# Two layers of attention and product-key experts: the expert gathers take the first four heads first, beside the selection of the other four

## The chip, the cores and the metric

One core of a Trainium2 chip runs the whole model. The metric is the time of one execution in device microseconds (us). The kernel before took 1806.02 us, the median of three runs between 1805.1 and 1806.14 us. TensorE is called PE (its weight loads PEld), VectorE DVE, ScalarE ACT, GpSimd POOL and SyncE SP; SP issues the weight loads, POOL the gathers.

## The reference

The input is one sequence of 256 tokens of 1024 numbers; 16 learned meta tokens are put ahead of it, so 272 tokens pass through two layers. A layer is a mixer (a causal convolution beside latent attention, merged by gates) and then a product-key expert layer:

```python
def _peer(h, wq, keys, u_table, v_table):          # h: 272 tokens after an RMS norm
    q = (hf @ wq).reshape(T, PEER_HEADS, 2, PEER_HALF)          # 8 heads, 2 halves of 128
    s = jnp.einsum('thpd,hpnd->thpn', q, keys)                  # 128 scores per half
    sv, si = lax.top_k(s, 16)
    cand = sv[:, :, 0, :, None] + sv[:, :, 1, None, :]          # 256 pairs
    top_s, top_pos = lax.top_k(cand.reshape(...), 16)           # 16 experts per head
    eidx = take(si[..., 0, ...] * 128 + si[..., 1, ...], top_pos)
    gw = softmax(top_s)
    # for each token its 128 experts:
    a = einsum('ted,td->te', u_table[eidx], x);  act = gelu(a) * gw
    out = einsum('te,ted->td', act, v_table[eidx])
```

There are 16384 experts, each a row of 1024 fp32 numbers in u_table and one in v_table, for each layer. The output is the 256 tokens without the meta tokens.

## The kernel before

**Stages.** In each layer the mixer comes first. Then 16 query tiles are made (the loop over i at L906): PE makes the queries and the scores, and DVE runs the top-16 (`top16`, L763) tile by tile beside it. The second selection (`second`, L807) turns the two sorted lists of a head into its 16 experts: a small table of candidate sums, a top-16 of it, a softmax on ACT, the place of each winner turned into a pair of list positions (L851 to L868, "pairs"), and two passes that look up the key numbers by those positions (L878 to L884, into `ef`). `heads(k, b)` (L887) does this for token block k (two blocks of 128 tokens) and heads 4b to 4b+3.

**Dense stages U and V.** 160 of the tokens are done densely. Stage U multiplies them by all 16384 rows of u_table: 128 stripes j of 128 experts, 8 matmuls of 128x160 each (`A<-xh,wraw`, which stand as 16 instructions on PE, two for an fp32 matmul); ACT and DVE turn `A` to the gated activation. Stage V multiplies by v_table, 128 stripes (`po<-X,wraw` and `po<-Xh,wraw`), accumulating the output. A weight tile of 1 MB holds two stripes; SP loads the tiles into a ring of four, and five tiles of U are loaded ahead during the query tiles (`we`). The last four stripes of V are done column block c by column block c (the tail); in layer 1 `turn_out` transposes each finished block and sends it out.

**Routes.** The gates of the dense tokens are a matrix of 160 tokens by 16384 experts, built on PE from one-hot matrices. The generator `routes` (L1045) makes their input beside U: w16 and its remainder at L1059 to L1061, and four transposes of `ef` on PE at L1072 for each token block k; `heads(1, 0)` and `heads(1, 1)`, the selection of the second token block, stand in it ("the second selection" below, whose transposes PE has in its queue at a fixed place). Then `wbuild` makes 40 blocks of `wp<-ohE,ohA`.

**Gathers.** The other 96 tokens, and in layer 0 the 16 meta tokens, are done by gathers. They stand in groups of 64, 32 and 16 tokens; a job is one expert of two heads for each of 64 tokens (of four heads for 32, of all eight for 16), 128 rows in all, so that there are 64 + 32 + 16 = 112 jobs in layer 0 and 96 in layer 1. `gather(k)` issues one indirect DMA from POOL (L1154): 128 rows of 8 KB, a u row and a v row of each expert, 1.05 MB into one of 4 buffers `gb`; its row numbers come from `iww`, which `spread` (L1035) writes from `ew` with a small DMA on POOL. Then DVE multiplies the u part by x with a running sum (L1182), ACT takes the gelu (L1192), DVE multiplies by the gate weight (L1161) and adds the v part times it (L1166), and the freed buffer takes the next gather. At the end `sum_heads` (L1024) sums the heads by PE with a matrix `zs`, and `put_back` adds to the residual `hT`.

**What sets the order.** Each engine executes its own instructions in the order in which the program is written. The two generators are advanced stripe by stripe: `routes` and `wbuild` by RB or RW[l] steps per stripe, the gathers by RU[l] steps per stripe of U from stripe J0 on (three steps per job), and in V by `rv`. In V a copy of one number of the newest weight tile (L1153, `warm`) stands ahead of each gather on POOL, so that a gather is issued no earlier than that tile has landed.

Of the kernel before, what the change touches and what calls it, by code (L numbers as in the profile page):

```python
# [7 lines left out]
F32 = mybir.dt.float32  # L8
# [11 lines left out]
META = 16  # L20
# [27 lines left out]
def trunk_kernel(ctx: ExitStack, tc: tile.TileContext, a: dict, out: bass.AP, dbg=None, stop=None):  # L48
# [135 lines left out]
    for l in range(NL):  # L184
# [622 lines left out]
        def second(v_, i_, nh, scale, iv, tsd):  # L807
# [47 lines left out]
            V.tensor_scalar(q3, po, 3, None, op0=OP.logical_shift_right)
            V.tensor_scalar(q2, po, 2, None, op0=OP.logical_shift_right)
            V.tensor_copy(nf, po)
            V.tensor_scalar(a_, q3, -1.0, 0.0, op0=OP.add, op1=OP.max)
            V.scalar_tensor_tensor(a_, q2, -5.0, a_, op0=OP.add, op1=OP.max)
            V.scalar_tensor_tensor(a_, nf, -42.0, a_, op0=OP.add, op1=OP.max)  # L860
# [116 lines left out]

        toks = [(META + sum(GROUPS[l][:g]), n) for g, n in enumerate(GROUPS[l])] + ([] if last else [(0, 16)])
# [17 lines left out]
        iww = [gp.tile([128, max(n // 16, 1), 2, min(n, 16)], F32, name=f"iww{i}") for i, (_, n) in enumerate(toks)]  # L996
        am = [gp.tile([128, max(n // 16, 1), min(n, 16)], F32, name=f"am{i}") for i, (_, n) in enumerate(toks)]
        zs_ = [gp.tile([128, n], F32, name=f"zs{i}") for i, (_, n) in enumerate(toks)]
        for z_, (_, n) in zip(zs_, toks):
            V.tensor_reduce(z_, ident.rearrange("p (t h) -> p t h", t=n), axis=AX.X, op=OP.add)  # L1000
# [34 lines left out]
        def spread(g):  # L1035

            q0, n = toks[g]
            s_ = done["e"][q0 - META:q0 - META + n]
            if n < 16:
                for q in range(2):  # L1040
                    G.dma_start(iww[g][:, 0, q], s_[:, :, q])
            else:
                G.dma_start(iww[g], s_)

        def routes():  # L1045
            done["e"] = ohp["ew"]
            spread(0)
            done["g"] = 1
            yield
            r2 = ohp["r"]  # L1050
            for k in range(2):
# [7 lines left out]
                V.tensor_scalar(h8(wh_), ts, WS, None, op0=OP.mult)  # L1059
                V.tensor_copy(ef[:, 2], wh_)  # L1060
# [82 lines left out]
        def gathers():  # L1143
# [52 lines left out]
            yield  # L1196
            yield
            sum_heads(len(toks) - 1)
            yield
            put_back(len(toks) - 1)  # L1200
# [56 lines left out]
        left = 3 * nj + 4 - done["n"]  # L1257
# [132 lines left out]
```

## Time and profile before

| | |
|---|---|
| median of 3 runs | 1806.02 us (1805.1 to 1806.14) |
| profiled execution | 1805.74 us, span 1804.0 us, mean granted clock 0.992 |
| PE busy | 1763.3 us, 98% |
| DVE busy | 1147.6 us, 64% |
| ACT, POOL busy | 422.7 us (23%), 329.3 us (18%) |
| U of layer 0 starts, V of layer 0 ends | 304 us, 928 us |
| U of layer 1 starts | 1202.65 us |
| DMA queue of the weights (q1), of the gathers (q0) | 338.54 MB, 218.35 MB |

The span is the time from the first to the last recorded instruction; the execution's own time is 1.7 us more. A PE that shows busy is not PE at its peak: matmuls whose weights come late are recorded as longer. The rows below are read with their columns as the line ahead of each group says; "[2.97 <-DVE ef L884]" means that the engine stood idle for 2.97 us and that DVE's instruction at L884 which writes `ef` ended it.

### The profile page before, as it was taken

What the parts mean: (1) busy time and instruction counts of PE and PEld (TensorE: products, weight loads), DVE (VectorE), ACT (ScalarE), POOL (GpSimd) and SP (SyncE); (2) the same over time, 40 slices, a digit from 0 to 9 for tenths busy, and PEclk for the clock granted to TensorE, in tenths of its full rate; (3) what the DMA queues carried; (4) which work ended last, traced back from release to release, by engine and by line L of the source; (5) the groups of instructions that cost most, each with busy time, mean ns of one, the idle gap of its engine ahead of it and who ended that gap; (6) DMA issues with size and microseconds to landing.
All of it is one profiled execution on the core that took longest, in us unless ns stands there. A gap on an engine that the chain in (4) does not pass through costs nothing.

```text
span 1804.0 us, 29548 instructions
## 1 busy us (share of the span) xinstructions
PE 1763.3 (98%) x11611; PEld 1627.8 (90%) x11611; DVE 1147.6 (64%) x3155; ACT 422.7 (23%) x1257; POOL 329.3 (18%) x393
## 2 busy tenths in 40 slices
PE   9999999989999999999999999999999999999998
PEld 7677888989999889988996878899899999999998
DVE  5577358997898654454535774587878886444341
ACT  3343112334444100000024331132344431000000
POOL 0121010222111223222200220102211122222220
PEclk9999999989999999999999999999999999999999
DMA  6223454889999999999962224658899999999994
GB/s 229 71 94 105 151 212 173 331 339 422 420 420 421 420 421 415 421 421 409 422 247 76 94 94 149 239 198 343 335 421 421 420 420 416 420 413 413 393 419 157
DMA packets 80684, 559.38 MB, mean 310 GB/s; under 512 B 9177, under 2 KB 12121, under 8 KB 13081
## 3 DMA queue, kind: packets, MB, share of 16 engines
q1 hardware_dynamic: 49488, 338.54, 47.5%
q0 software_dynamic: 30336, 218.35, 29.7%
q8 instruction: 91, 1.49, 0.3%
q10 hardware_dynamic: 720, 0.60, 0.1%
q14 instruction: 49, 0.39, 0.1%
HBM read 556.18 MB, written 1.05 MB: 309 GB/s over the span
## 4 chain that ended last, share of the span: by engine, by line
PE 72%; DMA 15%; DVE 7%; issue 5%; POOL 1%; ACT 0%; SPq 0%; DVEq 0%; POOLq 0%; ACTq 0%
PE po L56 23%; PE z L56 21%; PE A L56 19%; DMA wraw<-vn 10%; PE aps L56 5%; DMA wraw<-u 3%; PE wp L56 2%; DMA gb<-uv,iww 1%; DVE va L1166 1%; DVE gb L1182 1%; DVE ex L883 1%; DMA iww<-ew 0%; PE xp L56 0%; DMA wraw<-w_in 0%; DVE ex L880 0%
## 5 line engine op out<-in xcount | busy, mean ns | idle before, releaser
L56 PE MATMUL A<-xh,wraw 128*128 128x160 f32 x3776 | 540.6, 302 | 3.4 <-DMA wraw<-u 2.1
L56 PEld LDWEIGHTS A<-xh,wraw 128*128 128x128 f32 x3776 | 521.2, 191 | 6.4 <-DMA wraw<-u 3.4
L1182 DVE SCALAR_TENSOR_TENSOR gb<-gb,xr 128x1024 f32<-128x1024 f32 x208 | 254.6, 1224 | 344.3 <-DMA gb<-uv,iww 343.9
L56 PE MATMUL z<-xg,wraw 128*128 128x272 f32 (+1 forms) x1408 | 337.3, 394 | 0.8 <-DMA wraw<-w_in 0.7
L56 PEld LDWEIGHTS z<-xg,wraw 128*128 128x128 f32 x1408 | 265.4, 192 | 58.5 <-issue 7.5
L1154 POOL DMA_INDIRECT gb<-uv,iww x208 | 218.4, 1050 | 542.1 <-DVE va L1166 382.4
L56 PE MATMUL po<-Xh,wraw 128*128 128x160 f32 x2080 | 289.9, 300 | 9.3 <-DMA wraw<-vn 6.9
L56 PEld LDWEIGHTS po<-Xh,wraw 128*128 128x128 f32 x2080 | 283.4, 190 | 14.6 <-DMA wraw<-vn 11.2
L56 PE MATMUL po<-X,wraw 128*128 128x160 f32 x2016 | 280.3, 300 | 7.0 <-DMA wraw<-vn 5.6
L56 PEld LDWEIGHTS po<-X,wraw 128*128 128x128 f32 x2016 | 274.5, 190 | 12.3 <-DMA wraw<-vn 10.6
L1166 DVE SCALAR_TENSOR_TENSOR va<-gb,am,va 128x1024 f32<-128x1024 f32 x203 | 261.2, 1287 | 7.2
L1192 ACT ACTIVATE am<-am 128x1 f32<-128x1 f32 x208 | 41.4, 199 | 595.5 <-DVE gb L1182 595.3
L1093 ACT ACTIVATE ohA<-ohE,wlo 128x128 f16<-128x128 f16 x320 | 105.4, 427 | 7.8 <-DVE ohE L1090 5.6
L593 POOL TENSOR_TENSOR acc<-acc,cp 128x272 f32<-128x272 f32 (+1 forms) x60 | 51.1, 852 | 276.7 <-ACT cp L592 274.4
L1153 POOL COPY warm<-wraw 1x1 f32<-1x1 f32 x91 | 41.1, 452 | 289.3 <-DMA wraw<-vn 289.2
L585 DVE SCALAR_TENSOR_TENSOR acc<-upad,cols,acc 128x272 f32<-128x272 f32 (+1 forms) x180 | 83.8, 523 | 0.2
L1090 DVE TENSOR_TENSOR ohE<-ioh,idxT 128x512 f16<-128x512 f16 x160 | 60.4, 419 | 0.0
L56 PE MATMUL z<-xh,wraw 128*128 128x272 f32 (+1 forms) x256 | 57.3, 386 | 0.0
L56 PEld LDWEIGHTS z<-xh,wraw 128*128 128x128 f32 x256 | 48.6, 190 | 8.3
L1104 ACT ACTIVATE Xh<-wp 128x260 f32<-128x260 f32 (+17 forms) x80 | 25.7, 321 | 118.7 <-DVE Xh L1101 96.5
L56 PE MATMUL wp<-ohE,ohA 128*128 128x128 f16 x640 | 49.7, 218 | 0.0
L56 PEld LDWEIGHTS <-ohA 128*128 128x128 f16 x640 | 43.3, 97 | 3.0
(310 smaller groups left out, 1401.7 us busy)
## 6 DMA issues: line engine op xcount, KB each, us to landing
wraw<-vn SPq DMA_DIRECT2D x128, 1024.0 KB
wraw<-u SPq DMA_DIRECT2D x118, 1024.0 KB
wraw<-w_in SPq DMA_DIRECT2D x27, 1024.0 KB
wraw<-wq SPq DMA_DIRECT2D x16, 1024.0 KB
we<-u SPq DMA_DIRECT2D x10, 1024.0 KB
wraw<-w_out SPq DMA_DIRECT2D x8, 1024.0 KB
wraw<-w_mla SPq DMA_DIRECT2D x4, 1024.0 KB
wraw<-w_conv SPq DMA_DIRECT2D x4, 1024.0 KB
```

The lines of the kernel that those rows point to most:

```text
L56: PE.matmul(o, l, r, start=start, stop=stop, skip_group_check=True)
L585: V.scalar_tensor_tensor(acc[:, c, t0:], u_, weight(c, k), acc[:, c, t0:], op0=OP.mult, op1=OP.add)
L593: G.tensor_tensor(acc[:, 0, t0:], acc[:, 0, t0:], u_[:, t0:], op=OP.add)
L883: V.tensor_tensor(e3[:, :, 0:n], e3[:, :, 0:n], e3[:, :, n:2 * n], op=OP.add)
L1090: V.tensor_tensor(E[q], ioh[:, None].to_broadcast(full), pairs(q, b), op=OP.is_equal)
L1093: S.activation(A_[1][:, t // 2, :, t % 2], E[0][:, t // 2, :, t % 2], AF.Copy, scale=wlo[:, 4 * b + t:4 * b + t + 1])
L1104: S.activation(x_, p[:, :, a:b].rearrange("p t j -> p j t"), AF.Copy, scale=1.0 / WS)
L1153: G.tensor_copy(warm[0:1], state["w"][0:1, 0:1])
L1154: G.indirect_dma_start(out=g_, out_offset=None, in_=a[f"uv{l}"], in_offset=bass.IndirectOffsetOnAxis(ap=iww[i].bitcast(I32)[:, m // 16, 0, ...
L1166: V.scalar_tensor_tensor(vac[i], r, m_, vac[i], op0=OP.mult, op1=OP.add)
L1182: V.scalar_tensor_tensor(u_, u_, 1.0, xrs[i], op0=OP.mult, op1=OP.mult, accum_out=m_)
L1192: S.activation(m_, m_, AF.Gelu_apprx_tanh)
```

## The change

- The address list `iww` becomes permanent and is written in halves. Heads 0 to 3 (`numbers(.., 0)`, `spread(0, 0)`) are written ahead of the last scores. The rows of a job are arranged anew, so that the first half of a group's jobs (0 to 31 of the first 64) needs these heads only, the second half heads 4 to 7.
- `heads(0, 1)`, the eight small DMAs of the meta tokens (mv, mi), the addresses of heads 4 to 7 and four late top-16 (`behind`) move into `routes`, beside U.
- J0 goes from 8 to 3, RB from 0.75 to 0.85, RW from (0.52, 0.47) to (0.54, 0.5).
- The pairs are computed in ten DVE instructions instead of seventeen, on fp16.
- The gate multiply of a job goes from DVE to ACT, w16 and its fp32 copy too. The `zs` sums are made once at the start.
- The gathers are spread to the end of V, the last three stripes before the tail taking a job each. The last `sum_heads` and `put_back` stand in the tail ahead of block 5 (layer 0) or 1 (layer 1). `turn_out` of a block comes one block later.

```diff
-J0 = 8
+J0 = 3
-RB = 0.75
-RW = (0.52, 0.47)
+RB = 0.85
+RW = (0.54, 0.5)
...
-            V.tensor_copy(ab[0].rearrange("p h s -> p (h s)"), a_)
-            V.tensor_scalar(m, a_, 1.0, None, op0=OP.add)
-            V.scalar_tensor_tensor(m, a_, 2.0, m, op0=OP.mult, op1=OP.min)
-            w = ts
-            for d in (5.0, 17.0, 42.0):
-                V.tensor_scalar(w, a_, d, None, op0=OP.add)
-                V.scalar_tensor_tensor(m, m, 2.0, w, op0=OP.mult, op1=OP.min)
-            V.tensor_tensor(ab[1].rearrange("p h s -> p (h s)"), nf, m, op=OP.subtract)
...
+            W_.scalar_tensor_tensor(m, a_, 1.0, a_, op0=OP.min, op1=OP.add)
+            W_.scalar_tensor_tensor(m, m, 4.0, m, op0=OP.min, op1=OP.add)
+            W_.scalar_tensor_tensor(m, m, -4.0, nf, op0=OP.mult, op1=OP.add)
+            W_.tensor_scalar(b_, m, 0.0, None, op0=OP.max)
...
+        def numbers(ew, ef, x):
+            h4 = lambda q: ef[:, q, 64 * x:64 * x + 64].rearrange("p (h s) -> p h s", h=4)
+            V.scalar_tensor_tensor(ew.bitcast(I32)[:, 4 * x:4 * x + 4, 0], h4(0), 128.0, h4(1), op0=OP.mult, op1=OP.add)
+        def spread(g, x):
+            q0, n = toks[g]
+            G.dma_start(iww[g][:, n // 32 * x:n // 32 * (x + 1)], ohp["ew"][q0 - META:q0 - META + n, 4 * x:4 * x + 4])
...
+        run_all(early)
+        numbers(ohp["ew"], ohp["ef"], 0)
+        spread(0, 0)
         scores(15, pend)
-        if not last:
-            mv = rpool.tile([128, 1, 2, 16], F32, name="mv")
...
-                    G.dma_start(d4, s_[32 * q:32 * q + 16])
-        run_all(early)
-        run_all(heads(0, 1))
...
-        top16(behind[0:1])
-        top16(behind[1:2])
-        top16(behind[2:3])
-        top16(behind[3:4])
...
         def routes():
-            done["e"] = ohp["ew"]
-            spread(0)
+            r2 = ohp["r"]
+            if not last:
+                mv = rpool.tile([128, 1, 2, 16], F32, name="mv")
...
+                        G.dma_start(d4, s_[32 * q:32 * q + 16])
+            yield from heads(0, 1)
+            numbers(ohp["ew"], ohp["ef"], 1)
+            spread(0, 1)
+            for g in range(1, len(GROUPS[l])):
+                spread(g, 0)
+                spread(g, 1)
             done["g"] = 1
             yield
+            for b_ in behind:
+                top16([b_])
+                yield
...
-                V.tensor_scalar(h8(wh_), ts, WS, None, op0=OP.mult)
-                V.tensor_copy(ef[:, 2], wh_)
+                S.activation(h8(wh_), ts, AF.Copy, scale=WS)
+                S.activation(ef[:, 2], wh_, AF.Copy)
...
-                V.tensor_mul(m_, m_, iww[i][:, m // 16, 1, s_:s_ + 1])
...
                 S.activation(m_, m_, AF.Gelu_apprx_tanh)
+                S.activation(m_, m_, AF.Copy, scale=iww[i][:, m // 16, 1, m % 16:m % 16 + 1])
...
-        left = 3 * nj + 4 - done["n"]
         LJ = 128 - 2 * LASTP
-        rv = left / (LJ - 2)
+        tail = 3
+        rv = (3 * nj + 3 - done["n"] - 3 * tail) / (LJ - tail)
...
-            some_gathers(rv)
+            some_gathers(rv if j < LJ - tail else 3)
...
         for c in range(8):
+            if c == (1 if last else 5):
+                sum_heads(len(toks) - 1)
+                put_back(len(toks) - 1)
...
-                if c:
-                    turn_out(c - 1)
+                if c > 1:
+                    turn_out(c - 2)
                 V.tensor_add(hT[:, c, d0:], hT[:, c, d0:], pov[c])
         if last:
+            turn_out(6)
             turn_out(7)
```

POOL's queue at the start of U in layer 0. Before (mv and mi are the meta tokens' lists, iww0 the addresses of the first 64 tokens, gb a gather's buffer):

```order
L953 DMA mv_2102<-svm_1498 64x1x16 [waits DVE_49]
L953 DMA mi_2103<-sim_1499 64x1x16 [waits DVE_49]
L953 DMA mv_2102<-svm_1498 64x1x16
...
L1043 DMA iww0_2227<-ew_1823 128x1x128 [waits DMAHW1_49,DMAHW2_49,DMAHW0_49,DMAHW4_49,DMASW0_49,DMAHW7_49,DVE_49,Pool_49]
L1154 DMA gb_2260<-uv0,iww0_2227 128x2048 [waits DMASW1_49,DMASW0_49]
L1154 DMA gb_2262<-uv0,iww0_2227 128x2048 [waits DMASW2_49]
```

After, at the same place:

```order
L923 DMA iww0_1512<-ew_1832 128x1x64 [waits DVE_49]
L1043 DMA mv_2139<-svm_1504 64x1x16 [waits DVE_49]
L1043 DMA mi_2140<-sim_1505 64x1x16 [waits DVE_49]
...
L1158 DMA gb_2163<-uv0,iww0_1512 128x2048 [waits DMAHW2_49,DMAHW1_49,DMAHW4_49,DMAHW0_49,DMAHW7_49,DMASW1_49,Pool_49]
L1158 DMA gb_2165<-uv0,iww0_1512 128x2048 [waits DMASW2_49]
...
L923 DMA iww0_1512<-ew_1832 128x1x64 [waits DMASW5_49,DVE_49]
```

The first half of the addresses went ahead of the meta tokens' DMAs and the second half behind the first four gathers.

DVE's queue at the end of the selection of heads 4 to 7 of the first token block, in layer 0. Before (sv and si are top-16 lists):

```order
L883 TENSOR_TENSOR ex_2189<-ex_2189 128x4x32
L884 TENSOR_TENSOR ef_1822<-ex_2189 128x64
L958 SCALAR_TENSOR_TENSOR ew_1823<-ef_1822 128x8x16
L766 MAX sv_1496<-wlo_116 128x8
L768 MATCH_REPLACE idxT_115<-sv_1496,wlo_116 128x128
L770 MAX_INDEX si_1497<-sv_1496,wlo_116 128x8
```

After:

```order
L888 TENSOR_TENSOR ef_1831<-ex_2273 128x64
L1183 SCALAR_TENSOR_TENSOR gb_2163,am0_2116<-gb_2163,xr_2245 128x1024
L882 TENSOR_TENSOR ex_2289<-io16_96,ab1_2234 128x1024
...
L888 TENSOR_TENSOR ef_1831<-ex_2289 128x64
L918 SCALAR_TENSOR_TENSOR ew_1832<-ef_1831 128x4x16
L1183 SCALAR_TENSOR_TENSOR gb_2165,am0_2116<-gb_2165,xr_2245 128x1024
L1167 TENSOR_SCALAR va_2323<-gb_2163,am0_2116 128x1024
L771 MAX sv_1502<-wlo_122 128x8
```

Products of gathers now stand between the two look-up passes. Counted over DVE's whole queue of layer 0, 11 products stood ahead of the end of the second selection before and 17 stand there now; in layer 1 it was 11 and is 16.

PE's queue in U of layer 0, where the transposes of the second selection's ef stand. Before (stripes are 16 rows, A their sums):

```order
L56 MATMUL A_2919<-xh_1506,wraw_2718 128x160 x8
L56 MATMUL A_2919<-xh_1506,wraw_2818 128x160 x16
L1072 MATMUL wp_2953<-ident_89,ef_2517 128x128 x4
L56 MATMUL A_2961<-xh_1506,wraw_2855 128x160 x16
L56 MATMUL A_2961<-xh_1506,wraw_2904 128x160 x8
```

After:

```order
L56 MATMUL A_2977<-xh_1515,wraw_2858 128x160 x16
L56 MATMUL A_3012<-xh_1515,wraw_2915 128x160 x8
L1076 MATMUL wp_3023<-ident_89,ef_2626 128x128 x4
L56 MATMUL A_3012<-xh_1515,wraw_2915 128x160 x8
L56 MATMUL A_3012<-xh_1515,wraw_2958 128x160 x8
```

The four transposes moved from behind stripe 36 to behind stripe 43; in layer 1 from 37 to 44. The gather that comes last in layer 1 waits for the V tile of stripes 116 and 117.

## Rows read from the trace of the kernel before

**Rows 1.** Waits: engine, waiter, what ended it; total us, times, longest us.
```profile
DVE gb L1182 <- DMA gb<-uv,iww: 343.9, 155, 7.4
```

**Rows 2.** Windows of layer 0: us, each engine's busy us, PEclk, DMA share, GB/s.
```profile
304.00:313.00 9.00, 8.66 (x64) 8.69 (x65) 8.83 (x70) 2.92 (x6) 4.28 (x8) 1.00 0.54 210
313.00:327.00 14.00, 14.00 (x107) 14.00 (x106) 13.00 (x57) 0.62 (x1) 0.58 (x1) 1.00 0.70 236
327.00:345.00 18.00, 18.00 (x136) 18.00 (x135) 15.61 (x74) 10.83 (x19) 7.28 (x7) 1.00 0.92 370
345.00:400.00 55.00, 48.69 (x338) 47.82 (x337) 52.40 (x185) 17.50 (x37) 12.84 (x10) 0.91 0.89 335
...
500.00:600.00 100.00, 99.51 (x803) 97.46 (x803) 86.18 (x189) 38.90 (x138) 19.31 (x20) 1.00 1.01 420
...
901.00:928.00 27.00, 27.00 (x204) 27.00 (x203) 5.55 (x13) 3.00 (x7) 0.00 (x0) 1.00 0.59 220
```

**Rows 3.** Timeline of PE in V: start, us, instruction, count, idle before.
```profile
645.17 4.61 PE L56 MATMUL po<-X,wraw 128*128 128x160 f32 x32 [0.35 <-DMA wraw<-vn]
...
900.25 13.31 PE L56 MATMUL po<-Xh,wraw 128*128 128x160 f32 x96 [0.36 <-DMA wraw<-vn]
...
928.22 7.04 PE L56 MATMUL z<-xg,wraw 128*128 128x272 f32 x30
```

**Rows 4.** Timeline of POOL: the addresses and gathers of both layers.
```profile
311.44 0.61 POOL L953 DMA_DIRECT2D mi<-sim  x1
322.31 0.58 POOL L1043 DMA_DIRECT2D iww<-ew  x1 [10.26 <-issue]
327.40 1.03 POOL L1154 DMA_INDIRECT gb<-uv,iww  x1 [4.52 <-DMA iww<-ew]
...
883.08 0.96 POOL L1154 DMA_INDIRECT gb<-uv,iww  x1 [1.64 <-DVE va L1166]
...
888.04 0.96 POOL L1154 DMA_INDIRECT gb<-uv,iww  x1 [1.63 <-DVE va L1166]
...
1225.72 1.00 POOL L1154 DMA_INDIRECT gb<-uv,iww  x1 [3.54 <-DMA iww<-ew]
```

**Rows 5.** Timeline of PE at the second selection's transposes, both layers.
```profile
389.19 0.48 PE L1072 MATMUL wp<-ident,ef 128*128 128x128 f32 x1 [2.97 <-DVE ef L884]
392.13 0.80 PE L1072 MATMUL wp<-ident,ef 128*128 128x128 f32 x2 [2.46 <-DVE ef L1060]
392.72 9.00 PE L56 MATMUL A<-xh,wraw 128*128 128x160 f32 x48
...
1288.36 0.47 PE L1072 MATMUL wp<-ident,ef 128*128 128x128 f32 x1 [2.76 <-DVE ef L884]
1289.91 0.80 PE L1072 MATMUL wp<-ident,ef 128*128 128x128 f32 x2 [1.07 <-DVE ef L1060]
1290.50 11.14 PE L56 MATMUL A<-xh,wraw 128*128 128x160 f32 x64
```

**Rows 6.** Windows behind the stall of layer 0, columns as in rows 2.
```profile
390.00:396.00 6.00, 3.87 (x15) 3.73 (x16) 5.86 (x14) 1.41 (x5) 1.73 (x2) 0.50 0.83 315
396.00:399.00 3.00, 3.00 (x19) 3.00 (x18) 2.96 (x8) 1.36 (x5) 1.82 (x2) 0.76 0.63 213
```

**Rows 7.** Timeline of DVE, the first of the seventeen instructions of the pairs.
```profile
312.21 0.19 DVE L855 TENSOR_SCALAR q<-po 128x64 int32<-128x64 int32 x1
```

**Rows 8.** Groups by line: out<-in, count; busy us, mean ns; idle before.
```profile
L1161 DVE TENSOR_TENSOR am<-am,iww 128x1 f32<-128x1 f32 x208 | 32.2, 155 | 0.4 <-ACT am L1192 0.4
```

**Rows 9.** Timeline of DVE in layer 1: end of heads 0 to 3, first product.
```profile
1204.06 0.22 DVE L884 TENSOR_TENSOR ef<-ex 128x64 f32<-128x64 f16 x1
...
1234.37 1.23 DVE L1182 SCALAR_TENSOR_TENSOR gb<-gb,xr 128x1024 f32<-128x1024 f32 x1 [6.50 <-DMA gb<-uv,iww]
```

**Rows 10.** Timeline of PE in the tail of layer 1: the first and last of four.
```profile
1787.36 1.35 PE L56 MATMUL po<-Xh,wraw 128*128 128x160 f32 x8 [0.41 <-DVE hT L1298]
...
1797.96 1.35 PE L56 MATMUL po<-Xh,wraw 128*128 128x160 f32 x8 [0.69 <-DVE hT L1298]
```

**Rows 11.** Page: busy us, share of the span and instructions of each engine.
```profile
PE 1763.3 (98%) x11611; PEld 1627.8 (90%) x11611; DVE 1147.6 (64%) x3155; ACT 422.7 (23%) x1257; POOL 329.3 (18%) x393
```

More of the change, by code (lines that the diff above doesn't have):

```diff
@@ L141, in trunk_kernel @@
     V.memset(ec[0:8, 1:2], 0.0)
+    zs_ = {}
+    for n in (64, 32, 16):
+        zs_[n] = pp.tile([128, n], F32, name=f"zs{n}")
+        V.tensor_reduce(zs_[n], ident.rearrange("p (t h) -> p t h", t=n), axis=AX.X, op=OP.add)
     idxT = pp.tile([128, 3, 256], F16, name="idxT")
@@ L850, in second @@
             S.activation(tsd, ce, AF.Exp, scale=scale)
-            q3, q2, nf = rt("q3", [nh * 16], I32), rt("q2", [nh * 16], I32), rt("nf", [nh * 16])
-            a_, m = rt("ra", [nh * 16]), rt("rm", [nh * 16])
+            q3, q2 = rt("q3", [nh * 16], I32), rt("q2", [nh * 16], I32)
+            nf, m = rt("nf", [nh * 16], F16), rt("rm", [nh * 16], F16)
             ab = [rt(f"ab{p}", [nh, 16], F16) for p in range(2)]
[L855 to L860, printed above, removed]
-            V.tensor_copy(ab[0].rearrange("p h s -> p (h s)"), a_)
-            V.tensor_scalar(m, a_, 1.0, None, op0=OP.add)
-            V.scalar_tensor_tensor(m, a_, 2.0, m, op0=OP.mult, op1=OP.min)
-            w = ts
-            for d in (5.0, 17.0, 42.0):
-                V.tensor_scalar(w, a_, d, None, op0=OP.add)
-                V.scalar_tensor_tensor(m, m, 2.0, w, op0=OP.mult, op1=OP.min)
-            V.tensor_tensor(ab[1].rearrange("p h s -> p (h s)"), nf, m, op=OP.subtract)
+            a_, b_ = [x.rearrange("p h s -> p (h s)") for x in ab]
+            W_ = V
+            W_.tensor_scalar(q3, po, 3, None, op0=OP.logical_shift_right)
+            W_.tensor_scalar(q2, po, 2, None, op0=OP.logical_shift_right)
+            W_.tensor_copy(nf, po)
+            W_.tensor_scalar(a_, q3, -1.0, 0.0, op0=OP.add, op1=OP.max)
+            W_.scalar_tensor_tensor(a_, q2, -5.0, a_, op0=OP.add, op1=OP.max)
+            W_.scalar_tensor_tensor(a_, nf, -42.0, a_, op0=OP.add, op1=OP.max)
+            W_.scalar_tensor_tensor(m, a_, 1.0, a_, op0=OP.min, op1=OP.add)
+            W_.scalar_tensor_tensor(m, m, 4.0, m, op0=OP.min, op1=OP.add)
+            W_.scalar_tensor_tensor(m, m, -4.0, nf, op0=OP.mult, op1=OP.add)
+            W_.tensor_scalar(b_, m, 0.0, None, op0=OP.max)
             yield
@@ L905, in trunk_kernel @@
         early = heads(0, 0)
+        toks = [(META + sum(GROUPS[l][:g]), n) for g, n in enumerate(GROUPS[l])] + ([] if last else [(0, 16)])
+        iww = [pp.tile([128, n // 16, 2, 16], F32, name=f"iww{i}") for i, (_, n) in enumerate(toks)]
+        def numbers(ew, ef, x):
[4 more added lines that the diff above has]
+            G.dma_start(iww[g][:, n // 32 * x:n // 32 * (x + 1)], ohp["ew"][q0 - META:q0 - META + n, 4 * x:4 * x + 4])
         behind = []
@@ L976, in trunk_kernel @@
         n0 = 256 - N
-        toks = [(META + sum(GROUPS[l][:g]), n) for g, n in enumerate(GROUPS[l])] + ([] if last else [(0, 16)])
         xs_ = ExitStack()
@@ L994, in trunk_kernel @@
         xrs, vac = {}, {}
[L996 to L1000, printed above, removed]
+        am = [gp.tile([128, n // 16, 16], F32, name=f"am{i}") for i, (_, n) in enumerate(toks)]
         as2 = ExitStack()
@@ L1028, in sum_heads @@
             for c in range(8):
-                mm(done["p"][:, c], vac[i][:, c * 128:(c + 1) * 128], zs_[i], True, True)
+                mm(done["p"][:, c], vac[i][:, c * 128:(c + 1) * 128], zs_[n], True, True)
         def put_back(i):
@@ L1033, in put_back @@
             V.tensor_tensor(h_, h_, done["p"], op=OP.add)
[L1035 to L1043, printed above, removed]
-        def routes():
-            done["e"] = ohp["ew"]
-            spread(0)
+        def routes():
+            r2 = ohp["r"]
+            if not last:
+                mv = rpool.tile([128, 1, 2, 16], F32, name="mv")
+                mi = rpool.tile([128, 1, 2, 16], U32, name="mi")
+                for q in range(4):
+                    for d_, s_ in ((mv, svm), (mi, sim)):
+                        d4 = d_.rearrange("(n x) o s b -> x n o s b", x=2)[q // 2, :, 0, q % 2]
+                        G.dma_start(d4, s_[32 * q:32 * q + 16])
[5 more added lines that the diff above has]
+                spread(g, 1)
             done["g"] = 1
             yield
-            r2 = ohp["r"]
+            for b_ in behind:
+                top16([b_])
+                yield
             for k in range(2):
@@ L1169, in gathers @@
                 gather(k)
-            for g in range(1, len(GROUPS[l])):
-                spread(g)
             yield from x_steps(0)
@@ L1195, in gathers @@
             add(*prev)
[L1196 to L1200, printed above, removed]
         b_ = bg()
```

6 lines of the change are left out of this document (removed).

## The prediction

> **What bounds the kernel now.** I read the waits first. The largest wait that leads anywhere is VectorE's, 344 us over 155 products, for the rows of a gather to land [rows 1]. Then the windows of layer 0 from the start of stage U (304 us) to the end of V (928 us): in 500 to 600 us the DMA engines are fully used at 420 GB/s [rows 2]. The reader is to see that in these windows the engines are full from about 400 to 901 us and not full at both ends, at 210, 236, 370 and 335 GB/s ahead of it and 220 behind it. Third, the PE rows: while gathers run, two stripes of V cost 4.61 us and 0.35 us of waiting for a weight tile, without gathers six cost 13.31 us, 2.2 each [rows 3]. In 4.96 us one weight tile of 1.05 MB lands, 211 GB/s, and one gather of 1.05 MB is issued per 4.96 us [rows 4]: the two streams halve the 420. So layer 0 from 304 to 928 us is a number of bytes at 420 GB/s plus two stretches where too little is asked for. Layer 1 has 16 gathers fewer and no such full stretch early on; there PE is the bound, and only what idles PE counts.
>
> What delays the gathers is the fourth view. Their addresses, iww, were written at 322.31 us and the first was issued at 327.40 us in layer 0, at 1225.72 us in layer 1 [rows 4], because the selection of all eight heads stood ahead. Fifth, PE idles at the second selection's transposes: 2.97 and 2.46 us in layer 0, 2.76 and 1.07 in layer 1, always for VectorE's ef, and the 48 and 64 matmuls behind take 9.00 and 11.14 us instead of 6.6 and 8.8 [rows 5]. The granted clock there is 0.50, the 1.2 GHz level, in 390 to 396 us, and 0.76 in the next 3 us [rows 6].
>
> **Part 1, the early gathers in layer 0.** Against 420 GB/s the windows lack 9 x 210 = 1.89 MB, 14 x 184 = 2.58, 18 x 50 = 0.90 and 55 x 85 = 4.68 MB: together 10.05 MB, or 23.9 us of the DMA engines' time [rows 2]. After the change the addresses of heads 0 to 3 need only the first head group. The DMA that writes them is issued first on POOL; behind it, ahead of the first gather, stand the eight small DMAs of the 16 meta tokens, the last of which went out at 311.44 us and took 0.61 us [rows 4]. They keep their place because they wait for a top-16 that is not moved. So the first gather goes out at 312.1 us, 15 us earlier, and the window 313 to 327 looks like the present ramp of 327 to 345. Bounds for the saving: if everything from 327 us on stays as it is, the new deficit is 1.89 + 0.7 + 0.90 + 4.68 = 8.2 MB and 1.9 MB (4.5 us) is saved; if the engines are full from 313 us on, it is 1.9 MB and 8.2 MB (19.4 us) is saved. The order gives the middle: 17 products instead of 11 stand ahead of the end of the second selection. Six more gathers of 1.05 MB are 6.3 MB, 15.0 us. I take 15.0, the value nearest the order; it asks that VectorE does the six within about the same time. VectorE is busy 52.4 of 55 us in 345 to 400 [rows 2], so the six (about 2.7 us each with product and add) are paid from what goes: the three sums, two of three w16 steps, seven instructions of about 0.19 us in each of three calls of the pairs [rows 7], the gate multiply of 0.155 us per job [rows 8], some 7 us in all, and the idle time ahead of 345 us (1.0 + 2.4 us [rows 2]).
>
> The end of V gives the other part. Before, the last gather went out at 888.04 us [rows 4], the engines stayed full to 901 us, and 12 stripes were left from there to 928.22 us [rows 3] at 220 GB/s: 27 x 200 = 5.4 MB not asked for. After, the last gather waits for the tile of stripes 116 and 117. It is now issued with 17 stripes left (12 from 901 us, and about 5 in 13 us at 2.5 each), then with about 12: its rows land some 7 stripes from the end, about 17 us, a deficit of 3.4 MB. That saves at most 2 MB, 4.8 us; the last add, the sum over heads and its add now stand in the tail ahead of block 5 and may wait for it, so I take 3 us between 0 and 4.8. PE's stall in layer 0 is no term of its own: while PE stood, the ring of tiles filled and the engines' shortage is in the 4.68 MB. Layer 0: -18.0 us.
>
> **Part 2, layer 1.** Transposes of the second selection move from stripe 37 to 44. Without the waits PE would reach them at 1290.50 - 3.83 + 7 x 2.2 = 1302 us [rows 5]. VectorE: heads 0 to 3 are finished at 1204.3 us [rows 9]; from the issue of the addresses' DMA to the first gather it took 5.1 us in layer 0 (322.31 to 327.40), and from there to the first product 8.65 us in layer 1 (1225.72 to 1234.37) [rows 4, 9], so the first product can stand at 1218.0 us. The sixteenth is 15 x 4.96 us behind, and with 3 us, an estimate, for the selection's last steps the matrix is ready at 1295.4 us: 6.6 us ahead of PE. So the stall of 2.76 + 1.07 us and the half clock behind it, 11.14 - 8.8 = 2.4 us, go: -6.2 us, between 0 (it returns whole) and -6.2. What is late next is a weight tile: for 16 us more of the layer gathers take half of the engines. PE asks for 1.05 MB per 4.4 us, 239 GB/s, and gets 211, so 16 us of contention could cost 2 us; five tiles are loaded ahead, and I take +1 (0 to 2).
>
> The Trainium skill, DMA: Bandwidth & Descriptors, Queues, rings and completion order, says that a DMA engine takes turns between the queue rows it has work for, a packet at a time. By that rule a gather in flight costs the weight stream its half whatever the ring holds, and the full 2 us would be paid, with a sum of -24.2 instead of -25.2; the equal halves of rows 3 and 4 agree with it.
>
> **Part 3, the tail.** Four waits of PE for VectorE's adds, 0.41 to 0.69 us, stand in the last 13 us [rows 10]. With turn_out one block later the add has a block's matmuls of 1.25 us to hide behind: -2.4 us, and +0.4 for one more pair of transposes behind the last add. Bounds -2.8 and +1. The sum over heads only changes its place. The multiply by the gate weight moves from VectorE to ScalarE: 208 small instructions more on an engine that is busy 23% [rows 11], between a product and an add that comes one job later, so nothing.
>
> Sum: -18.0 - 6.2 + 1.0 - 2.0 = -25.2 us on the profiled execution of 1805.74 us (span 1804.0): 1780.5 us. Its time is 0.3 us under the median, so 1781 us.
>
> **Rivals.** A: VectorE stays full. It has 2.6 us of idle time in the 55 before 400 us [rows 2]; if the six extra gathers only push the second selection back, just the first bound holds (-4.5), the end gives -3, and layer 1 keeps its stall: -4.5 - 3 + 1 - 2 = -8.5, 1797 us. For it speaks the busy share, against it the 7 us removed.
>
> B: slower. Sixteen or seventeen jobs stand on VectorE's in-order queue ahead of the second selection instead of eleven, each held until its rows land, so at a landing interval d matrix and PE meet at 1218.0 + 15d + 3. At d = 4.96 nothing is lost. At d = 7 PE stands 24 us in layer 1, with the half clock 26.4 against 6.2: +20.2, and +19.2 with the other terms. In layer 0 seventeen jobs end at 312.1 + 8.65 + 16 x 7 + 3 = 436 us against PE at 392.72 - 5.4 + 15.4 = 403: 33 us in which only gathers of 150 GB/s flow lack 9 MB; the lack becomes some 14.6 MB against 10.05, +11 us less the 3 of the end. Together +27, 1833 us. It decides from about d = 6.2, where gains and losses cancel. Against it: the interval of 4.96 in rows 4 is one with both streams at work. For it: four gathers and a full ring ask at once in the first 30 us, where the rate has not been above 370 GB/s.
>
> C: the gathers start no earlier, because POOL's first gather is held by more than the eight small DMAs. Only the end and the tail remain: -3 - 2 and the stall partly back, -4 us, 1802 us. Against it stands the row at 311.44 us.
>
> **How the numbers follow.** Main case 0.71, A 0.15, B 0.09, C 0.05. The main case's own range is -12 (4.5 + 3 in layer 0, 5 in layer 1) to -34 (19.4 + 4.8, 9), 1772 to 1794 us. To hold 8 in 10 it takes in A and a little more: 1769 to 1799. A measurement of this kernel tells 0.2%, 3.6 us, from no change. Faster by more: 0.71 + 0.13 + 0.03, 0.87. Within: 0.04. Slower: 0.09.
>
> **What would show it.** Right: a first gather near 312 and 1209 us; over 330 GB/s in 313 to 345; U of layer 0 ending some 8 us earlier; the first z of layer 1 near 910 instead of 928 us; no idle PE above 0.5 us at the second transposes of layer 1, a clock of 1.00 behind them; no waits for hT in the tail. Wrong: a PE gap at the second transposes larger than before (B), the same deficits with an earlier first gather (A), a first gather at 327 us (C).

## The result and the profile after

The changed kernel takes 1779.43 us, the median of four runs from 1774.87 to 1785.35, against 1806.08 us for the kernel before on the same chip: a ratio of 0.9859 with a 95% interval of 0.9836 to 0.9882. Run again on another chip it took 1780.93 us, ratio 0.9863 (0.9848 to 0.9879). 1781 was forecast.

The profiled execution is the slowest of the four, 1785.35 us with a span of 1783.6. Read by stages from the first PE row of each, with the second run's profile (1781.19 us) beside it, in us:

| stage | before | after | after, again |
|---|---|---|---|
| start to U, layer 0 | 304.3 | 305.0 | 302.5 |
| U, layer 0 | 316.5 | 312.5 | 311.5 |
| V, layer 0 | 307.4 | 296.1 | 296.3 |
| mixer and queries, layer 1 | 274.4 | 276.1 | 276.1 |
| U, layer 1 | 309.9 | 304.3 | 303.4 |
| V and tail, layer 1 | 291.5 | 289.7 | 289.6 |

U and V of layer 0 give 15.3 and 16.0 us, those of layer 1 7.4 and 8.4. The stages ahead of U lie between 301.7 and 305.0 us over all the profiles of this study, the mixer of layer 1 between 272.7 and 276.1; these few us are no part of the change that can be told: the same kernel shows 305.0 and 302.5 us, and the last section says what they go with.

The windows of layer 0 in the profile after, with the columns of [rows 2], which they answer:

```profile
304.00:313.00 9.00, 8.42 (x62) 8.17 (x62) 8.83 (x70) 4.02 (x7) 5.92 (x10) 1.00 0.55 192
313.00:327.00 14.00, 14.00 (x107) 14.00 (x106) 9.95 (x27) 4.48 (x9) 4.88 (x6) 1.00 0.99 386
327.00:345.00 18.00, 18.00 (x135) 18.00 (x134) 13.45 (x49) 5.61 (x15) 3.91 (x4) 1.00 1.02 416
345.00:400.00 55.00, 55.00 (x409) 55.00 (x408) 51.49 (x192) 22.43 (x48) 10.58 (x10) 1.00 0.96 370
400.00:500.00 100.00, 95.42 (x758) 92.50 (x757) 80.75 (x166) 47.41 (x175) 23.17 (x21) 0.98 1.00 409
...
885.00:900.00 15.00, 14.65 (x108) 14.40 (x107) 7.01 (x9) 1.50 (x6) 1.85 (x2) 1.00 1.02 419
900.00:912.00 12.00, 11.59 (x88) 11.35 (x88) 5.31 (x11) 1.48 (x5) 0.00 (x0) 1.00 0.53 208
```

The engines are nearly full from 313 us instead of 400 us, and at the end only the last 12 to 14 us run at 208 GB/s. Not full is now 345 to 400 us, at 370 GB/s, and 400 to 500 us, at 409.

The timeline of POOL after, which answers to [rows 4], shows where the gathers start in both layers and where the last one of layer 0 goes out:

```profile
305.54 0.79 POOL L923 DMA_DIRECT2D iww<-ew  x1 [53.92 <-DVE sv L771]
...
311.74 1.05 POOL L1158 DMA_INDIRECT gb<-uv,iww  x1 [0.30 <-issue]
...
890.08 1.67 POOL L1158 DMA_INDIRECT gb<-uv,iww  x1 [0.56 <-DMA gb<-uv,iww]
...
1194.54 0.99 POOL L1158 DMA_INDIRECT gb<-uv,iww  x1 [1.99 <-DMA iww<-ew]
```

PE's timeline after, at the second selection's transposes ([rows 5] before) and at the first z of layer 1 ([rows 3]):

```profile
400.71 0.27 PE L1076 MATMUL wp<-ident,ef 128*128 128x128 f32 x1
402.89 0.44 PE L1076 MATMUL wp<-ident,ef 128*128 128x128 f32 x2 [1.90 <-DVE ef L888]
404.24 0.33 PE L1076 MATMUL wp<-ident,ef 128*128 128x128 f32 x1 [0.91 <-DVE ef L1065]
404.40 8.36 PE L56 MATMUL A<-xh,wraw 128*128 128x160 f32 x48
...
913.56 11.16 PE L56 MATMUL z<-xg,wraw 128*128 128x272 f32 x48
...
1287.53 0.60 PE L1076 MATMUL wp<-ident,ef 128*128 128x128 f32 x4
1287.97 6.69 PE L56 MATMUL A<-xh,wraw 128*128 128x160 f32 x48
```

In layer 1 PE no longer waits, and the 48 matmuls behind take 6.69 us; in layer 0 it still waits 1.90 and 0.91 us, and they take 8.36. In the tail, three waits of 0.20 us are left of the four of [rows 10]; this is the last of them:

```profile
1777.07 1.35 PE L56 MATMUL po<-Xh,wraw 128*128 128x160 f32 x8 [0.20 <-DVE hT L1299]
```

### The profile page after: what moved, and what is told of

The parts are those of the page before. It is cut to its first block, busy times and chain, and to the rows that moved or that the text cites. A ratio compares the mean times of both kernels' runs of the same rounds, so it can differ in the third digit from the quotient of the medians.

```text
span 1783.6 us, 29486 instructions
## 1 busy us (share of the span) xinstructions
PE 1755.8 (98%) x11611; PEld 1624.4 (91%) x11611; DVE 1102.8 (62%) x2886; ACT 480.7 (27%) x1464; POOL 336.4 (19%) x392
## 4 chain that ended last, share of the span: by engine, by line
PE 69%; DMA 12%; issue 9%; DVE 7%; POOL 3%; ACT 1%; SPq 0%; POOLq 0%; DVEq 0%; ACTq 0%
PE po L56 25%; PE z L56 24%; PE A L56 12%; DMA wraw<-vn 7%; PE aps L56 5%; DMA gb<-uv,iww 5%; POOL gb L1158 2%; DVE va L1169 1%; DVE gb L1183 1%; PE wp L56 1%; PE sc L56 1%; PE xp L56 0%; DVE ex L887 0%; DMA wraw<-w_in 0%; DVE ex L884 0%
## 5 line engine op out<-in xcount | busy, mean ns | idle before, releaser
L56 PE MATMUL A<-xh,wraw 128*128 128x160 f32 x3776 | 534.8, 301 | 1.2 <-ACT idxT L801 1.2
L1158 POOL DMA_INDIRECT gb<-uv,iww x208 | 228.0, 1096 | 533.3 <-DVE va L1169 375.9
L1157 POOL COPY warm<-wraw 1x1 f32<-1x1 f32 x86 | 36.5, 425 | 322.4 <-DMA wraw<-vn 322.3
L1194 ACT ACTIVATE am<-am,iww 128x1 f32<-128x1 f32 x208 | 61.5, 296 | 6.8
L1108 ACT ACTIVATE Xh<-wp 128x260 f32<-128x260 f32 (+18 forms) x80 | 25.0, 313 | 126.1 <-DVE Xh L1105 112.4
## 6 DMA issues: line engine op xcount, KB each, us to landing
wraw<-u SPq DMA_DIRECT2D x118, 1024.0 KB, 10.4
```

The lines of the kernel that those rows point to most:

```text
L56: PE.matmul(o, l, r, start=start, stop=stop, skip_group_check=True)
L1108: S.activation(x_, p[:, :, a:b].rearrange("p t j -> p j t"), AF.Copy, scale=1.0 / WS)
L1157: G.tensor_copy(warm[0:1], state["w"][0:1, 0:1])
L1158: G.indirect_dma_start(out=g_, out_offset=None, in_=a[f"uv{l}"], in_offset=bass.IndirectOffsetOnAxis(ap=iww[i].bitcast(I32)[:, m // 16, 0, ...
L1194: S.activation(m_, m_, AF.Copy, scale=iww[i][:, m // 16, 1, m % 16:m % 16 + 1])
```

## The experiments

The ratios are to the kernel before, measured beside each run. 0.9863 (0.9848 to 0.9879) is the changed kernel's, taken beside late_start, no_relief and old_end on one chip; the others came later, partly on another chip, so that ratios are compared and not only times. Each run takes something out of the changed kernel; none adds a part alone to the kernel before. Stages are compared with after_again.

**after_again.** No edit. 

> The changed kernel itself, beside the next three on one chip, since its four times lie 10 us apart. Both theories: 1774 to 1786 us, median 1780.

1780.93 us (1779.64 to 1781.5).

**late_start.** The selection of heads 4 to 7 ahead of U again, all addresses behind it.

```diff
+        scores(15, pend)
         run_all(early)
+        run_all(heads(0, 1))
         numbers(ohp["ew"], ohp["ef"], 0)
+        numbers(ohp["ew"], ohp["ef"], 1)
         spread(0, 0)
-        scores(15, pend)
+        spread(0, 1)
...
-            yield from heads(0, 1)
-            numbers(ohp["ew"], ohp["ef"], 1)
-            spread(0, 1)
```

> The changed kernel with one part undone: the selection of heads 4 to 7 stands ahead of stage U again, and the addresses are written after it, so the first gather goes out near 323 us instead of 312 in layer 0. Theory (layer 0 is a number of bytes at 420 GB/s, and the early gathers fill a stretch that is not full): the windows from 304 to 327 us lack 2 MB more, some 5 us, the stall in layer 1 may come back in part, 0 to 6 us: 1784 to 1792 us. Rival (VectorE's relief made the gain, not the start): within 3 us of the changed kernel.

1801.86 us, ratio 0.9979 (0.9968 to 0.9990): 21 us of the gain are gone, far more than expected. The selection's steps no longer stand in the routes, so PE's transposes moved forward to stripe 37, and there PE waited 11.14, 2.22 and 1.86 us for VectorE. So this run changes two things, the start of the gathers and the place of the transposes. The next kernel takes them apart.

**late_start_same_place.** As late_start, with six empty steps ahead of `done["g"] = 1`, which put the transposes back to stripes 43 and 44. 

> The late start once more, with six empty steps put into the routes, so that PE's transposes of the second selection stand at stripes 43 and 44 as in the changed kernel (in the run late_start they stood at 37 and 38, and PE idled 15 us there in layer 0). Theory (the late start itself lacks some 2.1 MB at 313 to 327 us, the rest of the 21 us was PE waiting at a place too early): no more than 3 us of idle PE at the transposes, U of layer 0 some 5 us longer than in the changed kernel, 1784 to 1788 us. Rival (the early gathers are worth nearly all by themselves): 1796 us or more.

1796.71 us, ratio 0.9952 (0.9937 to 0.9967). The rival held: 16 of the 21 us stay lost with the second selection's transposes at their place. The first gather goes out at 323.40 us in layer 0, 21.1 us behind the start of U, where after_again needs 6.7. U of layer 0 is 11.2 us longer, U of layer 1 8.4. The windows of this kernel show how:

```profile
313.00:327.00 14.00, 14.00 (x105) 14.00 (x104) 3.95 (x12) 1.75 (x2) 8.43 (x13) 1.00 0.73 258
327.00:345.00 18.00, 18.00 (x135) 18.00 (x134) 11.08 (x37) 2.73 (x10) 4.17 (x5) 1.00 0.99 397
345.00:400.00 55.00, 48.14 (x344) 47.90 (x343) 49.77 (x187) 23.63 (x51) 12.50 (x11) 0.94 0.94 356
```

VectorE, the third pair, is busy 3.95 us of the 14 from 313 us; in the changed kernel it was 9.95 and before 13.00. The products stand early in its queue now, and where the rows come late, all behind them stands still. The first product shows it:

```profile
329.12 1.22 DVE L1185 SCALAR_TENSOR_TENSOR gb<-gb,xr 128x1024 f32<-128x1024 f32 x1 [11.86 <-DMA gb<-uv,iww]
```

So the second selection is late, in layer 1 too, where PE waits again. And the late products hold ScalarE, whose gelus wait for them, so that PE finds a further wait in layer 0, at the transposes of the gathered tokens' x (L1022), which need the buffer that ScalarE's copy to wlo frees. The changed kernel has none there. First this row, then those of layer 1:

```profile
367.69 1.11 PE L1022 MATMUL wp<-ident,xs 128*128 128x128 f32 x4 [6.86 <-ACT wlo L1080]
...
1298.09 0.33 PE L1078 MATMUL wp<-ident,ef 128*128 128x128 f32 x1 [0.71 <-DVE ef L888]
1301.87 0.69 PE L1078 MATMUL wp<-ident,ef 128*128 128x128 f32 x2 [3.45 <-DVE ef L888]
1303.27 0.47 PE L1078 MATMUL wp<-ident,ef 128*128 128x128 f32 x1 [0.71 <-DVE ef L1067]
```

So the 16 us are not the price of the late rows' bytes alone. Of the 4.3 MB that the windows of layer 0 lack more than in after_again, 2.6 MB (6 us) lie ahead of 327 us and the rest behind, where PE waits. In layer 1 the waits at these transposes, 4.9 us and 1.75 more at L1022, are most of the 8.4.

**no_relief.** Pairs in seventeen steps, gate multiply and w16 on VectorE again.

```diff
...
-                S.activation(h8(wh_), ts, AF.Copy, scale=WS)
-                S.activation(ef[:, 2], wh_, AF.Copy)
+                V.tensor_scalar(h8(wh_), ts, WS, None, op0=OP.mult)
+                V.tensor_copy(ef[:, 2], wh_)
...
+                V.tensor_mul(m_, m_, iww[i][:, m // 16, 1, s_:s_ + 1])
...
-                S.activation(m_, m_, AF.Copy, scale=iww[i][:, m // 16, 1, m % 16:m % 16 + 1])
```

> The changed kernel with VectorE's work as before: pairs in seventeen instructions, gate multiply and w16 on VectorE. Theory: VectorE has some 7 us more work ahead of the second selection's end, so PE's idle time at its transposes in layer 0 grows from 2.8 to 6 to 10 us, but layer 0 is bound by bytes and loses 2 to 4 us, layer 1 0 to 2: 1781 to 1786 us. Rival A (VectorE full, its relief is the gain): 8 us or more, 1788 and above.

1788.13 us, ratio 0.9909 (0.9894 to 0.9923): 7 us by the times and 8 by the ratios. That is above the theory's range and at the lower edge of rival A's. U of layer 0 is 6.0 us longer than in after_again, U of layer 1 1.4. PE waits 7.2 us at the transposes of layer 0:

```profile
402.77 0.33 PE L1077 MATMUL wp<-ident,ef 128*128 128x128 f32 x1 [2.42 <-DVE ef L889]
406.79 0.48 PE L1077 MATMUL wp<-ident,ef 128*128 128x128 f32 x1 [3.69 <-DVE ef L889]
408.34 0.80 PE L1077 MATMUL wp<-ident,ef 128*128 128x128 f32 x2 [1.07 <-DVE ef L1065]
```

The stall was sized right (6 to 10 expected); that layer 0 would cover half of it was not. Of the 2.2 MB that the windows lack more than in after_again, 1.7 lie in 400 to 500 us (393 GB/s by 410), where PE waits; in 345 to 400 us the rate is 366 GB/s by 373.

**old_end.** The end of V and the tail as before.

```diff
             add(*prev)
+            yield
+            yield
+            sum_heads(len(toks) - 1)
+            yield
+            put_back(len(toks) - 1)
...
-        tail = 3
-        rv = (3 * nj + 3 - done["n"] - 3 * tail) / (LJ - tail)
+        rv = (3 * nj + 4 - done["n"]) / (LJ - 2)
...
-            some_gathers(rv if j < LJ - tail else 3)
+            some_gathers(rv)
...
-            if c == (1 if last else 5):
-                sum_heads(len(toks) - 1)
-                put_back(len(toks) - 1)
...
-                if c > 1:
-                    turn_out(c - 2)
+                if c:
+                    turn_out(c - 1)
...
-            turn_out(6)
```

> The changed kernel with the end of V and the tail as before (gathers done by stripe 122, sum over heads inside V, turn_out one block after). Theory: the last 27 us of layer 0 are at 220 GB/s again, 2.5 MB or 6 us, and the four waits in the tail of layer 1 are back, 2 us: 1786 to 1789 us, first z of layer 1 some 6 us later. Rival (the end of layer 0 hides the gathers anyway): 2 us from the tail, 1781 to 1783.

1786.19 us, ratio 0.9904 (0.9888 to 0.9920). V of layer 0 is 4.7 us longer than in after_again, V and tail of layer 1 1.8 us. As expected, in size too (6 and 2 us).

**four_jobs_fewer.** Four of the jobs of layer 0 left out.

```diff
+        if not last:
+            jobs = [x for x in jobs if not (x[0] == 0 and x[1] in (20, 30, 40, 50))]
```

> The changed kernel without four of the 112 gather jobs of layer 0 (their part of the output is missing). Theory (U and V of layer 0 are a number of bytes at 420 GB/s): 4 x 1.05 MB or 10 us less, 1769 to 1773 us, all of it between the start of U and the first z of layer 1. Rival (PE is the bound of these stages by now): at most 2 us, 1778 to 1781.

1772.33 us, ratio 0.9821 (0.9808 to 0.9834). U and V of layer 0 together are 9.3 us shorter than in after_again (10 expected), 8.3 in V and 1.0 in U. The gathers take a fixed number of steps per stripe of U, so that 60 products stand ahead of V here as in the changed kernel, and the four jobs fall out of V. So V of layer 0 is shown to be a number of bytes; U lost no job in this run.

**four_fewer_layer1.** The same four left out in layer 1 (`if last`). 

> The changed kernel without four of the 96 gather jobs of layer 1 (their part of the output is missing). Theory (layer 1 is bound by PE): at most 2 us less, 1779 to 1782 us, U and V of layer 1 as in the changed kernel within 1 us each. Rival (layer 1 is a number of bytes too): 10 us less, 1771 us.

1780.7 us, ratio 0.9874 (0.9858 to 0.9891), no change; U is 0.4 us shorter, V and tail the same to 0.1 us. Here too the jobs fall out of V (U keeps its 56 products), whose mean rate goes from 366 to 352 GB/s with no gain in time. So V of layer 1 is bound by PE. For U of layer 1 the run says nothing: in after_again the engines move 419 to 421 GB/s from 1300 to 1450 us, and still PE waits for no weight tile, so that both limits lie close together there.

**meta_behind.** A `yield` ahead of the meta tokens' DMAs, so that four gathers go first. 

> The changed kernel with the eight small DMAs of the meta tokens behind the first four gathers on POOL. Theory: the first gather goes out at 308 to 309 us instead of 311.7, 0.7 MB more by 313 us, 1 to 2 us: 1778 to 1780. Rival (the rows of the first gathers wait for VectorE, which is at heads 4 to 7 then): no change, 1780 to 1782.

1783.17 us, ratio 0.9870 (0.9854 to 0.9886): no change that can be told. The first gather went out at 306.48 us, 3.5 us behind the start of U instead of 6.7, and the windows show that the bytes gained were given back in 327 to 345 us:

```profile
304.00:313.00 9.00, 9.00 (x70) 9.00 (x69) 7.60 (x61) 2.50 (x4) 5.97 (x9) 1.00 0.63 239
313.00:327.00 14.00, 14.00 (x105) 14.00 (x105) 10.59 (x28) 7.41 (x15) 1.91 (x4) 1.00 1.01 423
327.00:345.00 18.00, 18.00 (x134) 18.00 (x133) 12.26 (x39) 3.26 (x9) 6.77 (x8) 1.00 0.90 346
345.00:400.00 55.00, 55.00 (x410) 55.00 (x409) 51.91 (x199) 23.75 (x49) 11.37 (x11) 1.00 0.96 386
```

Four buffers fill sooner, and the fifth gather goes out at 332.04 us, 7.8 us later than the 324.27 of after_again. What holds it is not VectorE, as the rival has it: POOL stands at three of the small DMAs, which come behind the four gathers now, 14.2 us in all, by the profile until a gather's rows have landed:

```profile
318.19 0.51 POOL L1044 DMA_DIRECT2D mi<-sim  x1 [4.28 <-DMA gb<-uv,iww]
324.00 0.50 POOL L1044 DMA_DIRECT2D mv<-svm  x1 [5.31 <-DMA gb<-uv,iww]
329.10 0.50 POOL L1044 DMA_DIRECT2D mi<-sim  x1 [4.60 <-DMA gb<-uv,iww]
...
332.04 1.01 POOL L1159 DMA_INDIRECT gb<-uv,iww  x1 [0.30 <-DMA mv<-svm]
```

**meta_behind_later.** The transposes of layer 0 at stripe 46 besides (two more empty steps for k = 1). 

> The same, and the second selection's transposes of layer 0 at stripe 46 instead of 43. Theory: PE's 2.8 us of waiting there and the half clock behind it go, the ring of weight tiles does not fill, 0.5 to 1 MB more by 420 us: 1775 to 1779 us. Rival (bytes alone bind, PE's wait is covered): as meta_behind within 1 us.

1785.68 us, ratio 0.9886 (0.9872 to 0.9901), no gain. The wait at the transposes is gone, and the one at the first one-hot block behind them is larger: 10.07 us, where meta_behind waits 2.11 and 0.96 us at the transposes and 4.29 at this block:

```profile
406.78 0.60 PE L1077 MATMUL wp<-ident,ef 128*128 128x128 f32 x4
407.21 6.69 PE L56 MATMUL A<-xh,wraw 128*128 128x160 f32 x48
423.97 1.03 PE L56 MATMUL wp<-ohE,ohA 128*128 128x128 f16 x8 [10.07 <-DVE ohA L1096]
```

**old_steps.** J0 8, RB 0.75, RW (0.52, 0.47). 

> The changed kernel with the step numbers as before (J0 8, RB 0.75, RW 0.52 and 0.47): the second selection's transposes of layer 0 move from stripe 43 to 47, the first one-hot block from 46 to 50, and 16 products instead of 17 stand ahead. Theory (VectorE's order decides, and a later place only moves the wait, as in meta_behind_later): the wait at the transposes is gone, that at the first one-hot block is 0 to 5 us, 1779 to 1785 us. Rival (the numbers are a part of the gain): 1788 us or more.

1786.35 us, ratio 0.9904 (0.9888 to 0.9921). That is 1.35 us above the theory's range and below the rival's; by the ratio it is 7 us over the changed kernel (the kernel before was 1803.23 us on this chip), which is the rival's edge. So neither is met, and the numbers count for some us. The wait at the transposes is gone, that at the first one-hot block is 3.62 us, as the theory has it. U of layer 0 is 2.2 us shorter, with two gathers fewer in it. V of layer 0, which takes these two, is 5.3 us longer in the profile; U of layer 1 is 5.4 us longer, and why was not tried.

**fewer_ahead.** The gathers of layer 0 slower up to stripe 45, then faster.

```diff
-                some_gathers(RU[l])
+                some_gathers(RU[l] if last else 1.3 if j < 46 else 1.53)
```

> The changed kernel with the gathers of layer 0 advanced by 1.3 steps per stripe up to stripe 45 and by 1.53 after, so that 15 products instead of 17 stand ahead of the second selection's end. Theory (VectorE's work ahead of the selection holds PE): two jobs of about 2.7 us less on VectorE, PE's 2.8 us of waiting at stripe 43 and the half clock behind it go, but the gathers of these two come later: 1777 to 1781 us. Rival (what is lost to the gathers in this stretch weighs more): 1783 us or more.

1784.84 us, ratio 0.9900 (0.9884 to 0.9917): the rival. PE waits no more at the transposes, but 2.87 us at the second one-hot block behind them; 345 to 400 us run at 355 GB/s instead of 373, and U of layer 0 is 4.6 us longer. The window of after_again, then that of this run:

```profile
345.00:400.00 55.00, 53.49 (x397) 53.23 (x395) 50.92 (x187) 21.79 (x47) 11.95 (x11) 1.00 0.97 373
...
345.00:400.00 55.00, 55.00 (x410) 55.00 (x410) 50.97 (x179) 20.70 (x45) 13.96 (x11) 1.00 0.93 355
```

Taken together, the bytes say where U of layer 0 lost its time. For each kernel the windows from 304 to 500 us are counted against 420 GB/s and their lacks added. This is an account and not a test of its own: U moves the same bytes, within 0.4 MB, in all kernels of the table but the last two, so a longer U must lack bytes somewhere. What it shows is that nearly all of the lack lies ahead of 500 us:

| kernel | lack, MB | against after_again, us at 420 GB/s | U of layer 0 against it, us |
|---|---|---|---|
| after_again | 6.0 | 0 | 0 (311.5) |
| meta_behind | 6.3 | +0.6 | +0.8 |
| meta_behind_later | 7.3 | +2.9 | +3.6 |
| no_relief | 8.2 | +5.2 | +6.0 |
| late_start_same_place | 10.4 | +10.3 | +11.2 |
| late_start | 11.5 | +13.0 | +13.2 |
| old_steps (two gathers, 5.0 us, fewer in U) | 6.8 | +1.9 - 5.0 | -2.2 |
| before (two gathers fewer in U) | 10.1 | +9.8 - 5.0 | +5.0 |

The one that doesn't follow is fewer_ahead (+1.3 by its lack of 6.6 MB, +4.6 measured). The 3.3 us between them stand at its end: PE waits 5.79 us for the last gelu ahead of V, which ScalarE has behind that of a gather, where after_again waits 2.53. V of layer 0 is 2.2 us shorter in turn. First this run, then after_again:

```profile
618.80 11.41 PE L56 MATMUL po<-X,wraw 128*128 128x160 f32 x61 [5.79 <-ACT gl L1218]
...
614.01 16.16 PE L56 MATMUL po<-X,wraw 128*128 128x160 f32 x117 [2.53 <-ACT gl L1218]
```

## Why the prediction was right, point by point

- **The time.** 1779.43 and 1780.93 us against 1781. That it came so near is in part luck: of the two terms of layer 0 one was too large and one too small.
- **The bound.** Right, and shown for V of both layers: four jobs fewer shorten layer 0 by 9.3 us of the 10 that their bytes cost at 420 GB/s, and layer 1 by 0.4. For U of layer 0 it rests on the account of bytes above; no run took a job alone out of U.
- **Early gathers, -15.0.** The mechanism is right and the term too large. The lack of 304 to 500 us fell from 10.1 MB (the 10.05 of the prediction and 0.1 behind 400 us) to 6.45 in the profile after and 6.0 in the second: 3.7 to 4.1 MB, 8.8 to 9.8 us. The count of six gathers, 15.0, gave too much: they stand ahead of the second selection in the order, but 345 to 400 us rose from 335 to 370 GB/s only, and not to 420. VectorE is busy 51.49 us of these 55 after and 52.40 before, as rival A feared; that it sets the rate there is likely and not shown. Every kernel that fed the engines more at one place of this stretch (meta_behind, fewer_ahead) lost it at another.
- **The relief of VectorE** stood in the prediction as cover only. The runs price it: 7 to 8 us. It isn't added to the 25 us, since without it the same products stand ahead of the same selection; neither are the 16 to 21 us of the late start. The parts need one another: undoing them one by one gives 7 to 8, 5 to 7 (old_end), some 7 (old_steps) and 16 or more, whose sum exceeds the whole. What each is worth alone, put into the kernel before, was not tried.
- **The end of V, -3.** Too small: the lack at the end fell from 5.4 MB to about 2.9 (212 x 12 us and the rest up to the first z), 6 us, and old_end measures 4.7 us. The wait of the tail for the last add, for which the term was taken lower, did not come. With 8.8 these are 15 us, as the stages give; -18.0 was forecast.
- **U ending 8 us earlier** was a wrong sign to look for: it ended 3.4 us earlier, at 617.46 (6.9 in after_again, 1.8 of them ahead of U). J0 puts two more jobs into U (60 instead of 58 products before V starts), 5 us of bytes that V then saves. V is 11 us shorter for that reason and for the end.
- **Layer 1.** The stall of 6.2 us went: U is 5.6 and 6.5 us shorter. The granted clock behind the transposes is 1.00 (1287 to 1296 us). The contention of +1 did not show: in the waits of the profile after no PE instruction of U of layer 1 waits for a weight tile, though the engines are nearly full from 1300 us on. So the equal halves of the two streams cost nothing there; that the tiles loaded ahead cover it is likely and was not tried. The first gather came 4.9 us behind the start of U, 6.8 forecast (1209.4 by 1202.65), so the selection was ready in time. The margin is smaller than the 6.6 us of the prediction: VectorE's last write of the second selection ends at 1283.96 us, and PE comes to it at 1287.53, 3.6 us later:

```profile
1283.68 0.28 DVE L1065 SCALAR_TENSOR_TENSOR ef<-ew,ef 128x128 f32<-128x128 f32 x1
```

- **The tail, -2.0.** Right: -1.8, though three waits of 0.20 us for hT are left where none was forecast.
- **Rival B** did not come about. It turned on the landing interval d, which came out at 5.3 us in layer 0 (17 products from 317.41 to 402.75 us) and 5.1 in layer 1 (16 from 1202.86 to 1278.70), against the 4.96 that the prediction took and the 6.2 at which B begins. What it describes, products ahead of the selection and PE waiting in both layers, is what late_start_same_place shows, by another cause: its interval is 5.1 and 4.9 us, but the first gather starts 14 to 15 us later behind the start of U.
- **Rival C** fell with the row at 311.74 us, against the 312.1 forecast.

## What to carry to other kernels

Where two DMA streams fill the engines, count the bytes that each window lacks against the full rate, and price a change by what it adds to them; a wait of another engine in that stretch costs the bytes that are not asked for meanwhile. An instruction moved forward in an in-order queue is worth its place only if its data come forward with it. And a wait that was stepped around was found again at a later consumer, 10.07 us of it at the first one-hot block in meta_behind_later and 2.87 us at the second in fewer_ahead.

## What the runs showed of the hardware

A small ACTIVATE with its scale from a column in memory takes 0.30 us, one without (the gelu) 0.20; the gate multiply that left VectorE at 0.155 us [rows 8] costs ScalarE twice that. The groups of ScalarE after, by line:

```profile
L1194 ACT ACTIVATE am<-am,iww 128x1 f32<-128x1 f32 x208 | 61.5, 296 | 6.8
L1193 ACT ACTIVATE am<-am 128x1 f32<-128x1 f32 x208 | 41.5, 199 | 597.0 <-DVE gb L1183 596.9
```

The changed kernel's first four times lie 0.6% apart, 1774.87 to 1785.35 us, its four on the second chip 0.1%, and before's fifteen on that chip 0.4%. Of the 4 us between its two profiles, 2.5 stand ahead of U in layer 0. These stages go with TensorE's granted clock. The mixer and queries of layer 1 took 272.7, 274.4 or 276.1 us in the thirteen profiles of this study, and in the 20 us that begin 60 us behind the first z the granted clock was 1.00, 0.91 and 0.83, in this order and without exception. The profile after and that of four_jobs_fewer show the two ends; in both PE waits 0.88 us for VectorE within this stretch, and the clock fell in one only (1.00 is 2.4 GHz):

```profile
973.56:993.56 20.00, 19.12 (x70) 14.40 (x71) 14.40 (x42) 4.53 (x9) 4.12 (x5) 0.83 0.29 105
...
963.10:983.10 20.00, 19.12 (x86) 15.21 (x87) 16.88 (x49) 5.68 (x14) 4.11 (x5) 1.00 0.28 106
```

The stages ahead of U in layer 0 do the same: 301.7 us with a clock of 1.00 in 80 to 100 us, 302.3 to 303.6 with 0.91, 304.3 to 305.0 with 0.83 or 0.84.
